# One-bank accumulators, a planner that counts descriptor space, and first weights by ScalarE in a two-layer trunk kernel

## The chip, the cores and the metric

The kernel runs on one core of a Trainium2 chip. The metric is the device time of one execution in microseconds (us), from several runs of the same program. Engines are called as the profile does: PE is the matrix engine (PEld its weight loads), DVE the vector engine, ACT the scalar engine, POOL GpSimd, SP the sync engine, which here only issues DMAs. PSUM is the accumulator memory: eight banks, of 512 f32 values in each of 128 partitions.

## What is computed

The reference is a trunk of two layers on x of 512 rows by 1024 columns in f32, each layer followed by a dense FFN, and a norm at the end:

```python
def sgu_mixer(h, w_in, w_s, b_s, ln_g, ln_b, w_out):
    z = jax.nn.gelu(h @ w_in)
    u, v = jnp.split(z, 2, axis=-1)
    v = layernorm(v, ln_g, ln_b)
    ...
    mixed = jnp.einsum('gts,bcsgd->bctgd', w, v)
    ...
    return (u * mixed) @ w_out

def retention(h, positions, w_in, gn_g, w_out):
    proj = h @ w_in
    q, k, v, g = jnp.split(proj, [RET_QK_WIDTH, 2 * RET_QK_WIDTH,
                                  2 * RET_QK_WIDTH + RET_V_WIDTH], axis=-1)
    ...
    return (o.astype(h.dtype) * jax.nn.silu(g)) @ w_out

def swiglu(h, w_gu, w_down):
    a, b = jnp.split(h @ w_gu, 2, axis=-1)
    return (jax.nn.silu(a) * b) @ w_down
```

Layer 0 mixes by sgu_mixer in chunks of 128 rows and 8 groups, layer 1 by retention with 4 heads, chunk by chunk. Every block reads an RMS-normed copy of x and is added back to x. The FFN's hidden width is 2816.

## The kernel before, in words

**Numbers.** Each f32 operand of a matmul is split in two parts of a shorter format: ACT makes the high part (names wh_, XH, xP7h), DVE the low part as the difference (wl_, XL, xP7l). A product is three matmuls: high by high, low by high, high by low. The large products use Strassen's scheme with seven block products, P1, P7, P6, Q4, P5, P2 and P3 (`seven`, L845). They need sums of weight blocks and sums of blocks of x. A raw weight block (wr_) is loaded by a DMA that SP issues. Where two blocks must be added, DVE does it, or GpSimd issues a second DMA that adds while it writes ("addition" below). Products are accumulated in PSUM under the names X, Y and Z: X_gu is accumulator X of the FFN's first product, X_dn of its second, X_so of the mixer's output product, X_qk and X_vg of retention's projections, X_ro of its output product, ps_v and X_u of the mixer's input products, mix of the spatial product.

**Stages in time.** The projection of v runs to 56 us, then u and the spatial mix to about 115, the mixer's output to 150, the first FFN to 480, retention to 840, the second FFN to 1182, and the last norm and store follow. At a block's opening, x is normed row chunk by row chunk (xs_), PE transposes it into PSUM (`turn`, L1204, tiles xT_), ACT copies the raw turned x (xr_, `raw_copy`, L1269) and its high part (XH_), DVE makes the low part and the sums of blocks, and xA (L1282) makes the high and low parts of those sums (xP7h, xP7l and so on).

**PSUM.** PS (L656) hands out one of four tiles of two banks, and done (L670) gives it back. A two-bank accumulator is written by PE in halves, c = 0 and c = 1, one bank each, and read by DVE or ACT either whole (128x1024) or by halves (128x512). The recorder counts a PSUM tile as one piece (L132, the grain): any write of any bank waits for every earlier read of the tile.

**The order.** No operation is issued when the code calls it. A Recorder (L211, L289: `record`) writes down every operation with its reads, writes and an estimated duration, and a planner (`order_of`, L430; `deadlines` and `forward` behind it) simulates the engines and two DMA lanes, one for SP's and ACT's transfers and one for GpSimd's. In the simulation each engine picks, among operations that are ready, the one that has to be done first; PE takes the lowest number. At most eight transfers per lane are in the air (HW_DMAS). Tiles come from pools with fixed numbers of buffers (N_GEN = 39, N_TMP = 5). The best of several rounds is emitted (L626), and each engine then runs its list strictly in order, with semaphores between engines. Since every operation is emitted by one line, all rows of the profile bear L341, and they are told apart by names.

**The head.** ACT issues one small load, SP the loads of x and of the first weights in turn (`open_w`, L1380). PE runs five warming matmuls on a constant tile (WAKE), then transposes the first block of x (`turn_in`, L1221) and begins with the projection of v (`open_step`, L1392, loop from L1406).

Of the kernel before, what the change touches and what calls it, by code (L numbers as in the profile page):

```python
# [15 lines left out]
P = 128  # L16
T = 512
# [4 lines left out]
KF = FF // P  # L22
HEADS = 4
GROUPS = 8
WAKE = 5
PREP = 5
FETCH = 8
ADD = 8
# [2 lines left out]
HIGH = 6  # L31
SUM = 7
N_GEN = 39
N_TMP = 5
SO = ("P1", "P7", "P6", "Q4", "P5", "P2", "P3")
UO = ("P1", "P7", "P6", "P2", "Q4", "P5", "P3")
U_DMA = ("P7",)
# [79 lines left out]
RESULT = 35  # L117
TO_PE = 55
HW_DMAS = 8


class Virtual:
# [72 lines left out]
        return n  # L195


class Pool:
    def __init__(self, rec, real, bufs, psum):
        self.rec, self.real, self.bufs, self.psum = rec, real, bufs, psum  # L200
# [4 lines left out]

class Op:
    __slots__ = ("n", "engine", "call", "before", "after", "tiles", "new", "busy", "took", "table", "kind", "start", "end",
                 "late", "left", "ready", "ins", "what", "slow", "then", "ahead", "open", "expect")


class Recorder:  # L211
# [11 lines left out]
    def add(self, engine, call, reads, writes, what, busy, took, table=None, kind=None, slow=0):  # L223
        op = Op()
        op.n, op.engine, op.call, op.what, op.busy, op.took, op.table, op.kind = len(self.ops), engine, call, what, busy, took, table, kind
        op.before, op.after, op.then, op.tiles, op.new, op.ins, op.slow, op.ahead = set(), [], [], [], [], None, slow, self.ahead
        seen = set()
        for views, w in ((reads, False), (writes, True)):
            for v in views:
                t, m = v.tile, v.mask()  # L230
                for q, qm, qw in t.history:
                    if q is not op and (w or qw or t.pool.psum and q.engine != engine) and qm & m:
                        op.before.add(q)
                if id(t) not in seen:
                    seen.add(id(t))
                    op.tiles.append(t)
                    t.users.append(op)
                    if t.first is None:
                        t.first = op
                        op.new.append(t)  # L240
                        if t.pool.psum:
                            was = self.held.get(t.tag)
                            self.held[t.tag] = t
                            op.before.update(was.users if was else ())
        for views, w in ((reads, False), (writes, True)):
            for v in views:
                t, m = v.tile, v.mask()
                if w:
                    t.history = [h for h in t.history if h[1] & ~m]
                t.history.append((op, m, w))  # L250
        for q in op.before:
            (q.then if q.engine == engine == "PE" else q.after).append(op)
        self.ops.append(op)
        return op
# [34 lines left out]
def record(self, attr, name, args, kwargs):  # L289
    args = [as_view(a) for a in args]  # L290
    kwargs = {k: as_view(a) for k, a in kwargs.items()}
    writes, reads = [], []
    if "out" in kwargs:
        writes.append(kwargs["out"])
    elif args:
        writes.append(args[0])
    if "accum_out" in kwargs:
        writes.append(kwargs["accum_out"])
    if "accum_op" in kwargs:
        reads.append(args[0])  # L300
    reads += [a for a in args[1:] if isinstance(a, View)]
    reads += [a for k, a in kwargs.items() if isinstance(a, View) and k not in ("out", "accum_out")]
    writes = [w for w in writes if isinstance(w, View)]
    engine = ENGINE_OF[attr]
    table = kind = None
    slow = 0
    n = writes[0].width() if writes else reads[0].width()
    psum = any(r.tile.pool.psum for r in reads)
    if name == "dma_start":
        kind = "add" if "accum_op" in kwargs else "load" if writes else "store"  # L310
        size = n * 4 * (writes or reads)[0].shape[0]
        busy = {"SP": 450, "POOL": 1200, "ACT": 450}[engine]
        took = busy
        slow = max(60, size * (SERVE_ADD if kind == "add" else SERVE) // 524288)
    elif name == "transpose":
        busy, took = 103, 275
    elif engine == "PE":
        n = args[2].width()
        busy = 4 * n // 2.4 if args[2].tile.dtype == F32 else max(60, n / 2.4 + (13.7 if n < T else 14.7))
        busy = int(busy + 0.0)  # L320
        took = busy + 166
    elif engine == "DVE":
        inputs = [r for r in reads if r.width() > 1 or n == 1]
        two = name in ("tensor_tensor", "scalar_tensor_tensor", "bn_stats") or psum
        busy = int(66 + (1.042 if two else 0.524) * (reads[0].width() if name == "bn_stats" else n))
        if name == "scalar_tensor_tensor" and isinstance(args[2], View):
            busy += 60
        took = busy + 84
    elif engine == "ACT":
        func = args[2]  # L330
        busy = int(90 + 0.835 * n) + (95 if "accum_out" in kwargs else 0)
        took = busy + 120 + (95 if "accum_out" in kwargs else 0)
        table = None if func in (AF.Copy, AF.Square) else str(func)
        if isinstance(kwargs.get("scale"), View):
            busy, took = int(88 + 1.03 * n), int(178 + 1.03 * n)
    else:
        busy = took = int(100 + 1.4 * n)
    fn = getattr(getattr(self.real, attr), name)

    def call():  # L340
        return fn(*[real_of(a) for a in args], **{k: real_of(a) for k, a in kwargs.items()})  # L341
    what = f"{name} {(writes or reads)[0].tile.name}"
    return self.add(engine, call, reads, writes, what, busy, took, table, kind, slow)
# [125 lines left out]
def forward(ops):  # L469
# [105 lines left out]
    while events:  # L575
# [7 lines left out]
        for e in queue:  # L583
            while busy_until[e] <= now:
                op = None
                if e == "PE":
                    op = min((o for o in queue[e] if can(o)), key=lambda o: o.n, default=None)
                else:
                    for o in queue[e]:
                        if can(o):  # L590
                            if o.kind:
                                fly = issued["sw" if e == "POOL" else "hw"]
                                if len(fly) >= HW_DMAS and (fly[-HW_DMAS].end is None or fly[-HW_DMAS].end > now):
                                    continue
                            cost = o.late + (3 * TABLE if o.table and o.table != table else 0)
                            if op is None or (cost, o.n) < best:
                                op, best = o, (cost, o.n)
# [35 lines left out]
def trunk(ctx, tc, x, positions, mix_g, ffn_g, fin_g, sgu_w_in, sgu_w_s, sgu_b_s, sgu_ln_g, sgu_ln_b,  # L633
# [19 lines left out]
    def TMP(name):  # L653
        return tmp.tile([P, T], F32, tag="t", name=name)

    ps_free = [0, 1, 2, 3]  # L656
    ps_held = []

    def PS(name, shape=(P, 2, T)):

        s = ps_free.pop(0)
        t = psp.tile(list(shape), F32, tag=f"ps{s}", name=name)
        ps_held.append((t, s))
        return t

    def done(*tiles):

        for t in tiles:
            i = next(i for i, (u, _) in enumerate(ps_held) if u is t)
            ps_free.append(ps_held.pop(i)[1])  # L670

    def f32(t):
        return t.bitcast(F32)
# [18 lines left out]
    onesr = const.tile([P, P], F32R, name="onesr")  # L692
    nc.vector.tensor_copy(onesr, ones)
    nc.scalar.activation(const.tile([P, 1], F32, name="first"), ones[:, 0:1], AF.Gelu_apprx_tanh)
    wake = PS("wake")
    flat = G("flat", F32R)
    nc.vector.tensor_copy(flat[:, 0, :].rearrange("p (c t) -> p c t", t=P), ones.view().rearrange("p (c t) -> p c t", c=1).to_broadcast([P, 4, P]))
    for _ in range(WAKE):
# [13 lines left out]

    def rows_to_cols(name):
        n = rows_in[name].shape[0]
        ps = PS(f"{name}_ps")
        nc.tensor.transpose(ps[:, 0, 0:n], rows_in[name], ident[0:n, 0:n])
        cols = const.tile([P, n], F32, name=f"{name}_cols")
        nc.vector.tensor_copy(cols, ps[:, 0, 0:n])
        done(ps)
        return cols  # L720
# [405 lines left out]
    def rows_of(cols, dst, name):  # L1126
# [2 lines left out]
        nc.vector.tensor_copy(ch, cols)  # L1129
        cl = small.tile([P, NC], F32R, tag="cl", name=f"cl_{name}")  # L1130
        nc.vector.tensor_tensor(cl, cols, f32(ch), ALU.subtract)
        ps = PS(f"rp_{name}")
        for i, part in enumerate((ch, cl)):
            dg = tmp.tile([P, NC, P], F32R, tag="t", name=f"dg{i}_{name}")
            nc.vector.tensor_tensor(
# [84 lines left out]

    def turn_in(c, j):  # L1221

        ps = PS(f"xT_in_{c}_{j}", (P, KD, P))
        for k in range(4):
            turned[c, j] = nc.tensor.transpose(ps[:, k, :], X[:, c, (4 * j + k) * P:(4 * j + k + 1) * P], ident)
        if (c, j) == (0, 0):
# [153 lines left out]
    def open_w(i):  # L1380
        wr = G(f"wr_v0_{i}")
        for a in range(2) if i < 2 else ():
            nc.sync.dma_start(wr[:, a, :], w_in[(2 * i + a) * P:(2 * i + a + 1) * P, D:D + T])
        if i >= 2:
            nc.sync.dma_start(wr, w_in[2 * i * P:(2 * i + 2) * P, D:D + T].rearrange("(a p) n -> p a n", p=P))
        wh, wl = G(f"wh_v0_{i}", F32R), G(f"wl_v0_{i}", F32R)
# [19 lines left out]
    for j in range(2):  # L1406
        for c in range(NC):
            if c == 0:
                open_w(2 * j)
            if (c, j) != (3, 1):  # L1410
                at = (c + 1) % NC, j + (c + 1) // NC
                load_x(*at)
            if c == 1:
                open_w(2 * j + 1)
            if (c, j) != (3, 1):
                turn_in(*at)
            open_step(c, 2 * j)
            if c == 1:
                open_step(0, 2 * j + 1)
            if c >= 1:  # L1420
                open_step(c, 2 * j + 1)
            if j == 1:
                square_in(c)
# [508 lines left out]
```

## Time and profile before

| what | value |
|---|---|
| time, median of 3 runs | 1189.12 us (1188.01 to 1190.46) |
| time of the profiled execution | 1190.77 us |
| its span, first to last instruction | 1189.1 us |
| mean granted clock of PE | 0.996 |
| instructions: PE, DVE, ACT, POOL | 7491, 1172, 851, 153 |
| bytes moved by DMA | 232.99 MB, 196 GB/s on the mean |
| additions (POOL's queue), share of 16 DMA engines | 74.72 MB, 37.7% |
| loads (SP's queue), share of 16 DMA engines | 156.80 MB, 40.3% |

The profiled execution took 1190.77 us by its own time, of which 1.67 us lie outside the span. It is 1.65 us above the median of the runs. The trace gives each instruction's start and duration, and for an engine that stood idle what ended the idle time: "[2.62 <-ACT xP7h_r]" is 2.62 us of idle before the instruction, ended by ACT's instruction that wrote xP7h_r. "issue" as a releaser means that the engine waited for nothing that the profile shows.

### The profile page before, as it was taken

Reading aid. Unit: us, or ns where it says so; the run is one execution under the profiler, and the core shown is the slowest. Engines: PE = TensorE matmul, PEld = TensorE weight load, DVE = VectorE, ACT = ScalarE, POOL = GpSimd, SP = SyncE. Lnnn points to the kernel's source line nnn. Section 1 sums busy time; section 2 is a strip of 40 time slices with the busy share of each in tenths; the row PEclk is TensorE's granted clock in tenths of the full one; section 3 lists DMA queues with packets and bytes.
Section 4 is the critical chain, followed back from the end, with each engine's and each line's share of the span. In section 5 each row is a group of like instructions: output and inputs, shape, how many; then the busy total and the mean of one; then the engine's idle time right before and its main releaser. Section 6 shows DMA issues by size and latency. Waiting matters only on the chain.

```text
span 1189.1 us, 18709 instructions
## 1 busy us (share of the span) xinstructions
PE 1172.1 (99%) x7491; PEld 1066.4 (90%) x7491; DVE 998.9 (84%) x1172; ACT 689.6 (58%) x851; POOL 177.9 (15%) x153
## 2 busy tenths in 40 slices
PE   9999999999999999899999999999999999999997
PEld 7899799989999988788989888888899989999986
DVE  6999999888779799898967678899988887665896
ACT  6445766456443558656656565567675545445474
POOL 1002121201101120211102011120121111011220
PEclk9999999999999999999999999999999999999999
DMA  9449988798856888869766788788897789669892
GB/s 327 114 126 207 310 183 215 167 240 211 214 143 155 192 186 277 193 143 234 163 169 174 162 213 197 168 166 260 240 217 178 166 225 228 180 170 241 177 228 80
DMA packets 132776, 232.99 MB, mean 196 GB/s; under 512 B 7592, under 2 KB 32208, under 8 KB 132688
## 3 DMA queue, kind: packets, MB, share of 16 engines
q1 hardware_dynamic: 91152, 156.80, 40.3%
q0 software_dynamic: 41376, 74.72, 37.7%
q8 instruction: 59, 0.97, 0.3%
q10 hardware_dynamic: 160, 0.27, 0.1%
q14 instruction: 29, 0.24, 0.1%
HBM read 228.61 MB, written 2.10 MB: 194 GB/s over the span
## 4 chain that ended last, share of the span: by engine, by line
PE 71%; DVE 8%; ACT 2%; issue 1%; DMA 1%; DVEq 0%; ACTq 0%
PE X_gu L341 19%; PE Y_gu L341 10%; PE X_dn L341 7%; PE X_vg L341 7%; PE Z_gu L341 4%; PE Y_dn L341 4%; PE X_qk L341 4%; PE Y_vg L341 4%; PE pv L341 2%; PE Y_qk L341 2%; PE Z_dn L341 2%; PE Z_vg L341 1%; DVE X L341 1%; PE sc L341 1%; PE X_ro L341 1%
## 5 line engine op out<-in xcount | busy, mean ns | idle before, releaser
L341 ACT ACTIVATE wh_gu_P<-wr_gu_P 128x1024 fp32r<-128x1024 f32 x132 | 137.3, 1056 | 128.6 <-DVE wr_gu_P L341 40.9
L341 DVE TENSOR_TENSOR wl_gu_P<-wr_gu_P,wh_gu_P 128x1024 fp32r<-128x1024 f32 x132 | 159.7, 1223 | 47.1 <-ACT wh_gu_P L341 39.0
L341 POOL DMA_DIRECT2D wr_gu_P<-in_ffn_w_gu x50 | 60.8, 1245 | 378.9 <-DVE wl_gu_P L341 179.2
L341 ACT ACTIVATE wh_dn_P<-wr_dn_P 128x1024 fp32r<-128x1024 f32 (+1 forms) x72 | 69.3, 983 | 45.7 <-PE Y_gu L341 8.7
L341 DVE TENSOR_TENSOR wl_dn_P<-wr_dn_P,wh_dn_P 128x1024 fp32r<-128x1024 f32 (+1 forms) x72 | 80.2, 1133 | 8.3 <-ACT wh_dn_P L341 7.7
L341 POOL DMA_DIRECT2D wr_dn_P<-in_ffn_w_down x40 | 46.4, 1191 | 173.7 <-DVE wl_dn_P L341 67.0
L341 DVE TENSOR_TENSOR wl_vg_P<-wr_vg_P,wh_vg_P 128x1024 fp32r<-128x1024 f32 x48 | 57.5, 1221 | 8.7 <-ACT wh_vg_P L341 7.6
L341 ACT ACTIVATE wh_vg_P<-wr_vg_P 128x1024 fp32r<-128x1024 f32 x48 | 49.1, 1060 | 18.7 <-DMA wr_vg_P<-in_ret_w_in 10.3
L341 POOL DMA_DIRECT2D wr_vg_P<-in_ret_w_in x26 | 32.1, 1310 | 137.1 <-DVE wl_vg_P L341 69.6
L341 PE MATMUL X_gu<-xP3h_f,wh_gu_P 128*128 128x256 f32 x176 | 50.4, 286 | 0.2 <-DVE s L341 0.2
L341 PE MATMUL Z_gu<-XH_f,wh_gu_P 128*128 128x256 f32 x176 | 50.0, 284 | 0.0
L341 PE MATMUL X_gu<-XH_f,wh_gu_P 128*128 128x256 f32 x176 | 49.9, 284 | 0.0
L341 PE MATMUL Y_gu<-xP7l_f,wh_gu_P 128*128 128x256 f32 x176 | 49.8, 283 | 0.0
L341 PE MATMUL X_gu<-xP6h_f,wh_gu_P 128*128 128x256 f32 x176 | 49.8, 283 | 0.0
L341 PE MATMUL X_gu<-xP6l_f,wh_gu_P 128*128 128x256 f32 x176 | 49.8, 283 | 0.0
L341 PE MATMUL X_gu<-xP6h_f,wl_gu_P 128*128 128x256 f32 x176 | 49.8, 283 | 0.0
L341 PE MATMUL Y_gu<-XL_f,wh_gu_Q 128*128 128x256 f32 x176 | 49.8, 283 | 0.0
L341 PE MATMUL Y_gu<-XH_f,wl_gu_Q 128*128 128x256 f32 x176 | 49.8, 283 | 0.0
L341 PE MATMUL Y_gu<-XH_f,wh_gu_Q 128*128 128x256 f32 x176 | 49.8, 283 | 0.0
L341 PE MATMUL X_gu<-xP5h_f,wh_gu_P 128*128 128x256 f32 x176 | 49.8, 283 | 0.0
L341 PE MATMUL Y_gu<-xP7h_f,wh_gu_P 128*128 128x256 f32 x176 | 49.8, 283 | 0.0
L341 PE MATMUL Y_gu<-xP7h_f,wl_gu_P 128*128 128x256 f32 x176 | 49.8, 283 | 0.0
(676 smaller groups left out, 4374.6 us busy)
## 6 DMA issues: line engine op xcount, KB each, us to landing
wr_gu_P<-in_ffn_w_gu SPq DMA_DIRECT2D x110, 512.0 KB, 5.9
wr_gu_P<-in_ffn_w_gu POOLq DMA_DIRECT2D x50, 512.0 KB, 7.9
wr_dn_P<-in_ffn_w_down SPq DMA_DIRECT2D x50, 512.0 KB, 5.7
wr_vg_P<-in_ret_w_in SPq DMA_DIRECT2D x40, 512.0 KB, 5.5
wr_dn_P<-in_ffn_w_down POOLq DMA_DIRECT2D x33, 512.0 KB, 8.1
wr_vg_P<-in_ret_w_in POOLq DMA_DIRECT2D x26, 512.0 KB, 8.1
wr_qk_P<-in_ret_w_in SPq DMA_DIRECT2D x20, 512.0 KB, 5.4
wr_ro_P<-in_ret_w_out SPq DMA_DIRECT2D x20, 512.0 KB, 6.1
```

The source lines that it names most:

```text
L341: return fn(*[real_of(a) for a in args], **{k: real_of(a) for k, a in kwargs.items()})
```

## The change

The change has six parts.

- **Accumulators of one bank.** PS now has eight one-bank tiles. A two-bank accumulator becomes a Pair of two tiles, and `record` splits each operation that has a Pair among its operands into two operations, one for each bank (`half_of` cuts the other operands). Tiles that never needed more take one bank: the warming tile, the small transposes, and xT_in.
- **Descriptor space.** The program is built with dynamic_dma_scratch_size 4096 instead of 2048.
- **The planner counts it.** Each transfer has a number `ring`: 2 if its last dimension is under 512, else 1. An addition isn't planned while its own number and those of the last seven that haven't finished 300 ns ago come to more than 7.
- **First weights by ScalarE.** The two loads of the first weight block are issued by ACT.
- **Order at the head.** The first step of the first product (`open_step(0, 0)`) is written ahead of the second block's transposes, and there are four warming matmuls instead of five.
- **Room.** N_TMP goes from 5 to 4 (2048 bytes of each partition).

In the built program DVE has 1248 instructions where it had 1174, ACT 869 where it had 803 (two of them DMA issues), SP 320 where it had 322; POOL's number is the same, PE has one matmul less. The diff, without the parts that only pass shapes:

```diff
-WAKE = 5
+WAKE = 4
...
-N_TMP = 5
+N_TMP = 4
...
+RING = 7
+FREED = 300
...
+def half_of(a, i, n):
+    if isinstance(a, Pair):
+        return a.parts[i].view()
+    if isinstance(a, View) and a.width() > 1:
+        assert a.shape[1] == n, (a.shape, n)
+        return a[:, i * n // 2:(i + 1) * n // 2]
+    return a
...
+        op.ring = 2 if kind and writes and writes[0].shape[-1] < T else 1
...
+    both = [a for a in (*args, *kwargs.values()) if isinstance(a, Pair)]
+    if both:
+        for i in range(2):
+            op = record(self, attr, name, [half_of(a, i, both[0].n) for a in args], {k: half_of(a, i, both[0].n) for k, a in kwargs.items()})
+        return op
...
+                                if e == "POOL" and o.ring + sum(q.ring for q in fly[-RING:] if q.end is None or q.end + FREED > now) > RING:
+                                    continue
...
-    ps_free = [0, 1, 2, 3]
+    ps_free = list(range(8))
...
-        s = ps_free.pop(0)
-        t = psp.tile(list(shape), F32, tag=f"ps{s}", name=name)
-        ps_held.append((t, s))
+        size = 1
+        for k in shape[1:]:
+            size *= k
+        banks = [ps_free.pop(0) for _ in range(size // T)]
+        if len(banks) == 1:
+            t = psp.tile(list(shape), F32, tag=f"ps{banks[0]}", name=name)
+        else:
+            t = Pair([psp.tile([P, shape[1] // 2, *shape[2:]], F32, tag=f"ps{b}", name=f"{name}_{i}") for i, b in enumerate(banks)])
+        ps_held.append((t, banks))
...
-            nc.sync.dma_start(wr[:, a, :], w_in[(2 * i + a) * P:(2 * i + a + 1) * P, D:D + T])
+            (nc.sync if i else nc.scalar).dma_start(wr[:, a, :], w_in[(2 * i + a) * P:(2 * i + a + 1) * P, D:D + T])
...
+            if (c, j) == (0, 0):
+                open_step(0, 0)
             if (c, j) != (3, 1):
                 turn_in(*at)
-            open_step(c, 2 * j)
+            if (c, j) != (0, 0):
+                open_step(c, 2 * j)
...
-    nc = bacc.Bacc("TRN2", target_bir_lowering=False, num_devices=1, dynamic_dma_scratch_size=2048)
+    nc = bacc.Bacc("TRN2", target_bir_lowering=False, num_devices=1, dynamic_dma_scratch_size=4096)
```

What the order of the built program shows of this at two places stands in the prediction, beside the sums that use it.

More of the change, by code (lines that the diff above doesn't have):

```diff
@@ L195, in width, with __init__, __getitem__ @@
         return n
+class Pair:
+    def __init__(self, parts):
+        self.parts = parts
+        self.n = 2 * parts[0].dims[1]
+    def __getitem__(self, key):
+        at, h = key[1], self.n // 2
+        if isinstance(at, int):
+            return self.parts[at // h][(key[0], at % h) + tuple(key[2:])]
+        a, b = at.start or 0, self.n if at.stop is None else at.stop
+        if a == 0 and b == self.n:
+            return self
+        i = a // h
+        assert (b - 1) // h == i, key
+        return self.parts[i][(key[0], slice(a - i * h, b - i * h)) + tuple(key[2:])]
+def half_of(a, i, n):
[5 more added lines that the diff above has]
+    return a
 class Pool:
@@ L207 @@
     __slots__ = ("n", "engine", "call", "before", "after", "tiles", "new", "busy", "took", "table", "kind", "start", "end",
-                 "late", "left", "ready", "ins", "what", "slow", "then", "ahead", "open", "expect")
+                 "late", "left", "ready", "ins", "what", "slow", "then", "ahead", "open", "expect", "ring")
 class Recorder:
@@ L669, in done @@
             i = next(i for i, (u, _) in enumerate(ps_held) if u is t)
-            ps_free.append(ps_held.pop(i)[1])
+            ps_free.extend(ps_held.pop(i)[1])
     def f32(t):
@@ L694, in trunk @@
     nc.scalar.activation(const.tile([P, 1], F32, name="first"), ones[:, 0:1], AF.Gelu_apprx_tanh)
-    wake = PS("wake")
+    wake = PS("wake", (P, 1, T))
     flat = G("flat", F32R)
@@ L714, in rows_to_cols @@
         n = rows_in[name].shape[0]
-        ps = PS(f"{name}_ps")
+        ps = PS(f"{name}_ps", (P, 1, T))
         nc.tensor.transpose(ps[:, 0, 0:n], rows_in[name], ident[0:n, 0:n])
@@ L1131, in rows_of @@
         nc.vector.tensor_tensor(cl, cols, f32(ch), ALU.subtract)
-        ps = PS(f"rp_{name}")
+        ps = PS(f"rp_{name}", (P, 1, T))
         for i, part in enumerate((ch, cl)):
@@ L1221, in turn_in @@
     def turn_in(c, j):
-        ps = PS(f"xT_in_{c}_{j}", (P, KD, P))
+        ps = PS(f"xT_in_{c}_{j}", (P, 4, P))
         for k in range(4):
```

## Prediction

> **What bounds the kernel now.** I read the page's busy row first, then the list of waits of the matrix engine, then the timeline round the longest waits. The page's first row, with busy time and share of the span by engine:
>
> ```profile
> PE 1172.1 (99%) x7491; PEld 1066.4 (90%) x7491; DVE 998.9 (84%) x1172; ACT 689.6 (58%) x851; POOL 177.9 (15%) x153
> ```
>
> PE is busy 1172.1 of 1189.1 us. The number of matmuls stays (one warming matmul goes), so the change can win only from the 17.0 us in which PE waits, and from stretches at a low clock; it loses wherever it makes PE wait anew. PE's waits, each with its total, count and longest:
>
> ```profile
> PE Y_qk L341 <- ACT xP7h_r L341: 2.6, 1, 2.6
> PE X_qk L341 <- ACT xP6h_r L341: 1.8, 1, 1.8
> PE wake L341 <- DVE flat L341: 1.7, 1, 1.7
> PE mix L341 <- DVE mx L341: 1.1, 1, 1.1
> PE X_so L341 <- DVE X L341: 0.8, 1, 0.8
> PE X_qk L341 <- ACT rq L341: 0.6, 1, 0.6
> PE X_dn L341 <- DVE X L341: 0.5, 1, 0.5
> PE xT_in L341 <- DMA X<-in_x: 0.4, 1, 0.4
> PE X_gu L341 <- DVE s L341: 0.2, 1, 0.2
> ```
>
> These nine make 9.7 us; of the remaining 7.3 nearly all is the tail behind PE's last matmul (the last row below, ended at 1182.0 of 1189.1). The worst place is the opening of retention, near 500 us. PE's timeline there:
>
> ```profile
> 494.03 1.03 PE L341 MATMUL xT_r<-ident,xs_r 128*128 128x128 f32 x8
> ...
> 503.14 0.58 PE L341 MATMUL Y_qk<-xP7h_r,wh_qk_P 128*128 128x256 f32 x1 [2.62 <-ACT xP7h_r L341]
> 505.54 0.58 PE L341 MATMUL X_qk<-xP6h_r,wh_qk_P 128*128 128x256 f32 x1 [1.82 <-ACT xP6h_r L341]
> 505.92 0.42 PE L341 MATMUL Y_qk<-xP7l_r,wh_qk_P 128*128 128x256 f32 x1
> ...
> 509.55 0.31 PE L341 MATMUL Y_qk<-xP7h_r,wh_qk_P 128*128 128x256 f32 x1
> 509.69 0.28 PE L341 MATMUL Y_qk<-xP7l_r,wh_qk_P 128*128 128x256 f32 x1
> ...
> 510.17 0.28 PE L341 MATMUL Y_qk<-xP7h_r,wl_qk_P 128*128 128x256 f32 x1
> ...
> 1181.65 0.39 PE L341 MATMUL W_dn<-wh_dn_P,h_P3l 128*128 128x512 f32 x1
> ```
>
> PE had turned x by 495.06 (first row), yet the high half of its sum, xP7h_r, came at 503.1. ACT's timeline, DVE's and GpSimd's say why:
>
> ```profile
> 499.19 1.06 ACT L341 ACTIVATE wh_vg_P<-wr_vg_P 128x1024 fp32r<-128x1024 f32 x1 [4.37 <-DMA wr_vg_P<-in_ret_w_in]
> 500.16 1.06 ACT L341 ACTIVATE xr_r<-xT_r 128x512 f32<-128x512 f32 x2
> ...
> 502.03 1.06 ACT L341 ACTIVATE xP7h_r<-xP_r 128x1024 fp32r<-128x1024 f32 x1
> ```
>
> ```profile
> 496.00 1.22 DVE L341 TENSOR_TENSOR wl_vg_P<-wr_vg_P,wh_vg_P 128x1024 fp32r<-128x1024 f32 x1
> 500.77 2.36 DVE L341 TENSOR_TENSOR xP_r<-xr_r,xr_r 128x1024 f32<-128x1024 f32 x2 [3.56 <-ACT xr_r L341]
> 503.17 1.23 DVE L341 TENSOR_TENSOR xP_r<-xP_r,xr_r 128x1024 f32<-128x1024 f32 x1
> 504.31 1.22 DVE L341 SCALAR_TENSOR_TENSOR xP7l_r<-xP_r,xP7h_r 128x1024 fp32r<-128x1024 f32 x1
> ```
>
> ```profile
> 484.07 1.76 POOL L341 DMA_DIRECT2D wr_vg_P<-in_ret_w_in  x1
> 490.21 1.22 POOL L341 DMA_DIRECT2D wr_vg_P<-in_ret_w_in  x1 [4.38 <-issue]
> ```
>
> ACT stood 4.37 us before a weight copy that needed an addition; the two copies of turned x (xr_r), queued behind it, had been ready for 5 us. That addition was issued at 490.21, after GpSimd had been held 4.38 us by something that the profile doesn't name ("issue"), following two additions at 483 and 484. The change counts a 256-wide addition as two units and holds one back when seven would be passed, with the space doubled; before, with half of that, 2+1 units were out. So I read the hold as descriptor space: an inference, not a row.
>
> The cost there is idle time and then clock:
>
> ```profile
> 500.00:504.00 4.00, 1.10 (x4) 0.38 (x2) 3.19 (x3) 3.92 (x6) 1.17 (x1) 0.85 0.96 178
> 504.00:508.00 4.00, 2.46 (x11) 2.46 (x12) 4.00 (x5) 3.15 (x4) 0.00 (x0) 0.50 0.96 204
> 508.00:512.00 4.00, 4.00 (x30) 4.00 (x29) 4.00 (x5) 1.51 (x3) 0.00 (x0) 0.80 0.02 3
> ```
>
> The columns are the stretch, its length, busy time of PE, weight load, DVE, ACT and POOL with counts, then granted clock, DMA share, GB/s: the clock falls to 0.85, 0.50, 0.80. From 505.92 to 509.55 there are 17 matmuls in 3.63 us, 0.214 each; at full clock four take 0.48 (509.69 to 510.17), 0.12 each. The loss is 17 x 0.094 = 1.6 us.
>
> **The change part by part.** *Retention's opening.* The new accounting makes the planner's order different. ACT before, from the first of the copies in question (xr_r copies of turned x, XH_r its high half, wh_ high halves of weights):
>
> ```order
> L341 ACTIVATE wh_vg_P_0_0_5180<-wr_vg_P_0_0_4979 128x1024
> L341 ACTIVATE wh_qk_P_0_0_5193<-wr_qk_P_0_0_4906 128x1024
> L341 ACTIVATE wh_vg_P_0_2_5208<-wr_vg_P_0_2_5020 128x1024
> L341 ACTIVATE xr_r_0_5160<-xT_r_5203 128x4x128
> L341 ACTIVATE xr_r_1_5167<-xT_r_5203 128x4x128
> L341 ACTIVATE XH_r<-xT_r_5203 128x8x128
> L341 ACTIVATE xP7h_r<-xP_r 128x1024
> ```
>
> And now, at the same place:
>
> ```order
> L377 ACTIVATE wh_qk_P_0_0_5292<-wr_qk_P_0_0_4962 128x1024
> L377 ACTIVATE wh_vg_P_0_0_5298<-wr_vg_P_0_0_5062 128x1024
> L377 ACTIVATE xr_r_0_5257<-xT_r_0_5310 128x4x128
> L377 ACTIVATE xr_r_1_5266<-xT_r_1_5315 128x4x128
> L377 ACTIVATE XH_r<-xT_r_1_5315 128x4x128
> L377 ACTIVATE xP7h_r<-xP_r 128x1024
> L377 ACTIVATE xP5h_r<-xP_r 128x1024
> L377 ACTIVATE xP6h_r<-xP_r 128x1024
> L377 ACTIVATE wh_vg_P_0_2_5366<-wr_vg_P_0_2_5118 128x1024
> ```
>
> The copy of the late weights has moved behind all three sums, so x no longer waits for an addition, however late. Next in line is DVE: with xr_r from 495.1 and DVE's low halves of weights done at 497.2, two sums of 1.18 end at 499.4 with xP7h ready 1.06 after the first; a third sum of 1.2 and xP7l's 1.2 end at 501.8. PE comes free at 500.5 (503.14 less 2.62) and its second matmul needs xP7l: 1.2 us stay, and of the wait for rq some 0.3. So 2.6 + 1.8 + 0.6 = 5.0 of idle plus 1.6 of clock are 6.6 now, and 1.5 remain: **-5.1**. If the late addition is still the last to come for a matmul behind it, up to 2.6 remain.
>
> Whether a gap of 1.2 us costs clock, the stretch with mix's gap of 1.1 tells (columns as above):
>
> ```profile
> 72.00:76.00 4.00, 3.48 (x30) 3.48 (x31) 4.00 (x6) 0.00 (x0) 0.00 (x0) 1.00 0.09 19
> ```
>
> The clock stayed at 1.00 there, while after 2.62 and 1.82 it did not. By the Trainium skill, "TensorE: Matmul & The Clock Gate", HAM oscillation, only gaps over about 3.4 us matter; here the clock fell in a stretch whose single waits were 2.62 and 1.82, so the row is stricter. By the page alone I could not have charged the first gap with any clock; the 1.6 us, and the sum, stay as measured.
>
> *One-bank accumulators.* A write to a two-bank tile had to wait for a read of its other bank. PE at X_so before, where the second bank (first row with "wh_so_P_0_0") begins:
>
> ```order
> L341 MATMUL X_so<-wh_so_P_0_2_1347,y_P3h_1369 128x512
> L341 MATMUL X_so<-wl_so_P_0_2_1375,y_P3h_1369 128x512
> L341 MATMUL X_so<-wh_so_P_0_2_1347,y_P3l_1420 128x512
> L341 MATMUL X_so<-wh_so_P_0_0_1322,y_P3h_1369 128x512
> L341 MATMUL X_so<-wl_so_P_0_0_1366,y_P3h_1369 128x512
> ```
>
> And now:
>
> ```order
> L377 MATMUL X_so_1171<-wh_so_P_0_2_1384,y_P3h_1397 128x512
> L377 MATMUL X_so_1171<-wl_so_P_0_2_1434,y_P3h_1397 128x512
> L377 MATMUL X_so_1171<-wh_so_P_0_2_1384,y_P3l_1408 128x512
> L377 MATMUL X_so_1182<-wh_so_P_0_0_1377,y_P3h_1397 128x512
> L377 MATMUL X_so_1182<-wl_so_P_0_0_1391,y_P3h_1397 128x512
> ```
>
> The order is the same; the second bank is a tile of its own, and nothing reads it while DVE adds the first to X. So X_so's 0.8, X_dn's 0.5 and X_gu's 0.2 go. Of mix's 1.1 I count half, 0.6, since DVE's own place for mx can keep the other half. **-2.1**; bounds 0 and -2.6.
>
> *Split instructions.* Built, DVE has 74 more and ACT 64 more (two first loads apart). Durations of whole and half:
>
> ```profile
> L341 DVE TENSOR_TENSOR X<-X,X_dn 128x1024 f32<-128x1024 f32 x9 | 10.9, 1217 | 5.5 <-PE X_dn L341 5.5
> L341 DVE TENSOR_TENSOR X<-X,X_dn 128x512 f32<-128x512 f32 x6 | 3.9, 685 | 0.0
> ```
>
> ```profile
> L341 ACT ACTIVATE y<-Y_gu 128x1024 f32<-128x1024 f32 x10 | 10.2, 1016 | 4.8 <-PE Y_gu L341 4.2 <-PE X_gu L341 0.6
> L341 ACT ACTIVATE rq<-X_qk 128x512 f32<-128x512 f32 x8 | 4.7, 590 | 2.0 <-PE X_qk L341 1.9
> ```
>
> Two halves cost 2 x 0.685 - 1.217 = 0.15 more on DVE, 74 x 0.15 = 11.3 us; on ACT 2 x 0.590 - 1.016 = 0.16, 64 x 0.16 = 10.5 us. DVE then stands at 1010 of 1189 us and ACT at 700, both below PE. DVE is full only in some stretches:
>
> ```profile
> 420.00:450.00 30.00, 30.00 (x134) 24.83 (x133) 29.96 (x30) 19.29 (x22) 5.44 (x5) 1.00 0.90 202
> 450.00:480.00 30.00, 30.00 (x146) 25.15 (x144) 29.32 (x44) 24.48 (x38) 1.32 (x1) 1.00 0.92 274
> ```
>
> In the sixty microseconds before 480 DVE has 0.72 us free and PE does not wait once: DVE prepares weights ahead there. The splits in it are few (by the program five additions of a sum to X), 0.8 us, which the free time about takes. So the splits lie beside PE's work; if the lead is used up, they surface. For new waits of this sort, and those of the altered order, I put in one bank read of 0.7: **+0.7**; bounds 0 and 2.6, as much as the short waits of today.
>
> *Head.* SP's first two weight loads go to ScalarE, one warming matmul goes, and the first step comes before the second turn.
>
> ```profile
> 1.26 0.90 SPq L341 DMA_DIRECT2D wr_v<-in_sgu_w_in  x2
> ```
>
> ```profile
> 5.40 0.63 ACT L341 ACTIVATE wh_v<-wr_v 128x512 fp32r<-128x512 f32 x1 [2.46 <-DMA wr_v<-in_sgu_w_in]
> 6.61 0.63 ACT L341 ACTIVATE wh_v<-wr_v 128x512 fp32r<-128x512 f32 x1 [0.58 <-DMA wr_v<-in_sgu_w_in]
> ```
>
> SP's queue is 0.90 us shorter for the x that follows, so at most 0.9 is won; but these landings are 1.2 apart, and a first weight that lands one place later costs 1.2. ACT's table load moves behind two issues and is covered by the 2.46 of waiting. **0**, bounds -0.9 and +1.2.
>
> *Tail:* its instructions stand as before. **0.**
>
> Sum on the profiled execution, whose time is 1190.77 (the span and 1.67 around it): -5.1 - 2.1 + 0.7 = -6.5, 1184.3. It lay 1.65 above the median of the runs, 1189.12; so I forecast **1182.6**. Bounds: the retention term -6.6 to -4.0, short waits -2.6 to 0, the new ones 0 to +2.6, the head -0.9 to +1.2 each move it alone; taken together, mostly not all at once, 1179 to 1187.
>
> **Rivals.** Differences within 0.2%, 2.4 us, count as no change.
>
> R1, *the stall stays in another dress*: the sums now wait for a chain of DVE work as long as the wait for the addition. For: DVE has four operations between xr_r and xP7l. Against: the rows give 501.8, not 505.5. Only the short waits are won, -2.1 + 0.7: 1187.7.
>
> R2, *all goes*: no residue at retention (-6.6), all short waits (-2.6), the head's 0.9: 1189.1 - 10.1 = 1179.0. For: the chain's residue shrinks if the additions come early and DVE's low halves with them.
>
> R3, *slower: transfers collide*. With twice the descriptors, GpSimd has up to seven additions in the air, against SP's loads on DMA engines that are already at a share of 0.90 to 0.96 in the stretches quoted. If SP's raw weights land later than the lead of the copies, ACT meets a late DMA ahead of something PE needs, as at 499.19, in other places. One such stall, 6.6 us, eats the gain (1189.2); it decides from two on: 1182.6 + 2 x 6.6 = 1195.8. Against: PE waits for a weight's DMA nowhere after the head, and the planner's lanes reckon with sharing.
>
> R4, *DVE becomes the bound*: half of its 11.3 us surface in the full stretches, 5.6: 1188.2. The Trainium skill, "VectorE: DVE Perf Modes", the errata section, says that each instruction pays a fixed extra cost whatever its size; the 0.15 of the rows agrees. Against: PE has no wait for a low half of a weight today.
>
> **How the numbers follow.** Forecast 0.58, R1 0.14, R2 0.11, R3 0.11, R4 0.06. Faster (below 1186.7): 0.58 + 0.11 and 0.02 of R1, 0.71. Slower (above 1191.5): 0.11. Same: 0.18. Forecast's own range is 1179 to 1187; down to R2 and up to R1 and R4 gives 1178.5 to 1188.8, which leaves R3 and edges out.
>
> **What would show it.** Right: in the list of PE's waits xP7h_r and xP6h_r are gone or make under 1.5 us, the clock near 500 us stays at 1.00, ACT's wait for wr_vg stands behind xP6h_r, and X_so and X_dn wait for no DVE X. DVE's busy time is near 1010. Wrong: a new wait of PE on ACT over 2 us, a second dip of the clock, rows of SP's loads with landing times well above those of today, or DVE's xP sums as late as 503.

## The result and the profile after

The changed kernel takes 1179.18 us on the median (six runs, 1177.65 to 1180.06), the kernel before 1189.05 beside it (six runs, 1185.58 to 1193.55): ratio 0.9914, 95% interval 0.9893 to 0.9935. The forecast was 1182.6. The profiled execution took 1179.72 us, its span is 1177.9.

All the waits that PE has left, as its list of waits gives them (total, count, longest), and the page's busy row:

```profile
PE wake L377 <- DVE flat L377: 1.7, 1, 1.7
PE ps_v L377 <- ACT wh_v L377: 0.9, 2, 0.5
PE xT_in L377 <- DMA X<-in_x: 0.9, 1, 0.9
```

```profile
PE 1167.4 (99%) x7490; PEld 1065.1 (90%) x7490; DVE 1009.1 (86%) x1246; ACT 694.3 (59%) x915; POOL 177.4 (15%) x153
```

Of the nine waits shown of before, the seven behind the head are gone, and none has come in their place. All three that are left lie in the first ten microseconds, where one has grown and one is new. DVE works 10.2 us more, about the 11.3 forecast; ACT 4.7 more, not 10.5.

At the opening of retention, ACT, GpSimd, DVE and PE in the timeline of the changed kernel:

```profile
492.32 1.09 ACT L377 ACTIVATE xr_r<-xT_r 128x512 f32<-128x512 f32 x2 [0.25 <-PE xT_r L377]
494.68 1.06 ACT L377 ACTIVATE xP7h_r<-xP_r 128x1024 fp32r<-128x1024 f32 x1 [0.79 <-DVE xP_r L377]
498.05 1.04 ACT L377 ACTIVATE wh_vg_P<-wr_vg_P 128x1024 fp32r<-128x1024 f32 x1
```

```profile
479.38 1.21 POOL L377 DMA_DIRECT2D wr_vg_P<-in_ret_w_in  x1
481.42 1.21 POOL L377 DMA_DIRECT2D wr_vg_P<-in_ret_w_in  x1 [0.83 <-DVE nf_dn L377]
```

```profile
493.43 2.35 DVE L377 TENSOR_TENSOR xP_r<-xr_r,xr_r 128x1024 f32<-128x1024 f32 x2
496.96 1.22 DVE L377 SCALAR_TENSOR_TENSOR xP7l_r<-xP_r,xP7h_r 128x1024 fp32r<-128x1024 f32 x1
```

```profile
491.69 1.03 PE L377 MATMUL xT_r<-ident,xs_r 128*128 128x128 f32 x8
498.01 0.28 PE L377 MATMUL Y_qk<-xP7h_r,wh_qk_P 128*128 128x256 f32 x1
498.24 0.39 PE L377 MATMUL Y_qk<-xP7l_r,wh_qk_P 128*128 128x256 f32 x1
```

ACT copies the turned x at once; the late weights come behind the sums and are copied without a wait. GpSimd's second addition isn't held. PE goes from Z_vg into Y_qk without a gap: xP7l is ready at 498.18, and the matmul that needs it starts at 498.24. The stretches that had a clock of 0.85 and 0.50:

```profile
500.00:504.00 4.00, 4.00 (x36) 4.00 (x35) 4.00 (x5) 3.22 (x6) 0.00 (x0) 1.00 0.90 221
504.00:508.00 4.00, 3.98 (x29) 3.41 (x28) 4.00 (x5) 3.25 (x5) 2.46 (x2) 1.00 0.45 51
```

To see where the time went, I laid PE's matmuls of the two traces beside each other by work done, the warming ones left out and each other one counted with its usual spacing in the traces (0.227 us for 512 columns, 0.12 for 256, 0.11 for 128), and read how much later the changed kernel is at the same amount of work:

| time before, us | changed kernel against before | step |
|---|---|---|
| to 20 | +2.4 | head |
| 20 to 69 | -0.5 | projection of v, first part of u |
| 69 to 76 | -1.5 | mix |
| 142 to 158 | -1.1 | X_so |
| 188 to 203 | -0.4 | X_gu |
| 474 to 490 | -0.9 | X_dn |
| 490 to 528 | -7.3 | opening of retention |
| 543 to 558, 845 to 861 | -0.6 | two small places |
| all else to PE's end | -1.2 | pieces of 0.15 or less |
| PE's end | -11.1 | 1182.0 against 1170.9 |

The rows sum to -11.1. The profiled executions differ by 11.05 us, the medians by 9.9, since the execution profiled of before was one of its longer ones.

### The profile page after: what moved, and what is told of

The parts are those of the page before. It is cut to its first block, busy times and chain, and to the rows that moved or that the text cites. A ratio compares the mean times of both kernels' runs of the same rounds, so it can differ in the third digit from the quotient of the medians.

```text
span 1177.9 us, 18861 instructions
## 1 busy us (share of the span) xinstructions
PE 1167.4 (99%) x7490; PEld 1065.1 (90%) x7490; DVE 1009.1 (86%) x1246; ACT 694.3 (59%) x915; POOL 177.4 (15%) x153
## 4 chain that ended last, share of the span: by engine, by line
PE 98%; ACT 1%; DMA 1%; DVE 0%; ACTq 0%; issue 0%; DVEq 0%
PE X_gu L377 22%; PE Y_gu L377 11%; PE X_dn L377 9%; PE X_vg L377 7%; PE Z_gu L377 5%; PE Y_dn L377 5%; PE ps_v L377 4%; PE X_qk L377 4%; PE Y_vg L377 4%; PE X_ro L377 4%; PE Z_dn L377 3%; PE pv L377 2%; PE Y_qk L377 2%; PE X_u L377 2%; PE X_so L377 2%; PE Y_ro L377 2%
## 5 line engine op out<-in xcount | busy, mean ns | idle before, releaser
L377 ACT ACTIVATE wh_vg_P<-wr_vg_P 128x1024 fp32r<-128x1024 f32 x48 | 49.7, 1056 | 10.2 <-DMA wr_vg_P<-in_ret_w_in 3.5
L377 PE MATMUL X_gu<-xP5h_f,wl_gu_P 128*128 128x256 f32 x176 | 49.8, 283 | 0.0
L377 PE MATMUL X_gu<-xP3l_f,wh_gu_P 128*128 128x256 f32 x176 | 49.8, 283 | 0.0
L377 PE MATMUL X_gu<-xP3h_f,wl_gu_P 128*128 128x256 f32 x176 | 49.8, 283 | 0.0
```

## The experiments

Theory: the stall at retention's opening needs both, an addition that comes late because descriptor space is full, and a planner's order that puts ACT's copy of these weights ahead of the copies of x; one-bank tiles end the short waits. Rivals: descriptor space alone carries the gain, or the counting does; and for the head, the early first step rather than ScalarE's loads. Each group of four runs shared a chip and its runs of the kernel before.

**Space and order apart (runs 1 to 3).** The kernel before, with nothing but its descriptor space changed; all its instructions stand in the same order:

```diff
-dynamic_dma_scratch_size=2048
+dynamic_dma_scratch_size=2560
```

> The kernel before, instruction for instruction, with descriptor space 2560 instead of 2048 (the most that fits beside its other buffers). If GpSimd's hold of 4.38 us near 486 us is descriptor space, one more addition fits: the addition that came at 490.2 comes near 486, ACT does not wait 4.37 us for it, PE's waits for xP7h_r and xP6h_r (2.6 + 1.8) fall below 1.5 together, the clock dip goes, and the time is 5 to 7 us under the kernel before. If the hold is something else (the rival: the order alone decides), all of this stays as before and the time is within 1 us of the kernel before.

Measured: 1185.65 us against 1188.72 for the kernel before on that chip (29 runs, 1183.4 to 1192.9), ratio 0.998 (0.9963 to 0.9997). GpSimd's timeline, and two of PE's waits:

```profile
485.56 2.44 POOL L341 DMA_DIRECT2D wr_vg_P<-in_ret_w_in  x2 [5.61 <-DVE wl_vg_P L341]
```

```profile
PE X_gu L341 <- ACT u L341: 2.0, 2, 1.0
...
PE X_qk L341 <- ACT xP6h_r L341: 1.1, 1, 1.1
```

Two additions now follow each other at once: the hold was descriptor space, as nothing else differs. The wait for xP7h_r is gone and that for xP6h_r is 1.1. Laid side by side by work done, PE gains 5.6 us from 490 to 528. Less than that shows in the times. The profiled execution is 2.6 below the one profiled before, since new or longer waits in the FFNs take back 3.1 us, of which the two for u make 2.4. The median is 3.1 below, since the kernel before doesn't always have the full stall: of its 29 runs here, the ten with a mean granted clock of 0.996 or less all took 1189.99 or more, and the ten with 0.998 or 0.999 took 1183.4 to 1186.5. In runs 1 to 3 none of the 30 executions is under 0.997.

The kernel before with only the pool of temporaries made smaller, with which the planner's order comes out with the late copy behind the sums of x:

```diff
-N_TMP = 5
+N_TMP = 4
```

> The kernel before with only N_TMP 4 instead of 5: descriptor space stays 2048, nothing is counted, banks and head as before. The planner's order then happens to have the late weight copy behind the three sums of x. If the order is what ends the stall, PE's waits for xP7h_r and xP6h_r make under 1.5 us while GpSimd is still held for about 4 us near 486, and the time is 5 to 7 us under the kernel before. The rival, that the addition's lateness matters wherever the copy stands, expects PE to wait 2 us or more for a part of wr_vg or a chain behind it, and a time within 2 us of the kernel before.

Measured: 1185.10, ratio 0.9979 (0.9961 to 0.9997). GpSimd's row and PE's wait:

```profile
491.88 1.22 POOL L341 DMA_DIRECT2D wr_vg_P<-in_ret_w_in  x1 [5.74 <-issue]
```

```profile
PE X_qk L341 <- ACT xP6h_r L341: 1.4, 1, 1.4
```

The hold is there, longer than before (5.74 against 4.38), and the stall is not: this order without more space is enough too. The prediction put the new order down to the counting; nothing was counted here, so it can come about without. The smaller pool may have moved other instructions as well; runs 11 and 12 move one alone. Both edits together:

```diff
-N_TMP = 5
+N_TMP = 4
-dynamic_dma_scratch_size=2048
+dynamic_dma_scratch_size=4096
```

> The same instructions in the same order as the run with N_TMP 4, with descriptor space 4096. If order alone ends the stall, the time is within 1 us of that run, and only GpSimd's hold near 486 goes. If space matters beside it (the rival), it is 2 us or more below that run.

Measured: 1185.26, ratio 0.9975 (0.9957 to 0.9992), the same as with the order alone. The wait for xP6h_r falls to 0.2 in the profiled execution, which the medians do not show. All three lie 3.1 to 3.6 us under the median of before, not 5 to 7: the mechanism came as expected, but the expected size was that of the execution profiled before, which had the full stall (run 3's profiled one, of 1184.50, is 6.3 below it), and not that of the median one.

**Head (runs 4 to 7).** The changed kernel with its head as before:

```diff
-WAKE = 4
+WAKE = 5
-            (nc.sync if i else nc.scalar).dma_start(wr[:, a, :], w_in[(2 * i + a) * P:(2 * i + a + 1) * P, D:D + T])
+            nc.sync.dma_start(wr[:, a, :], w_in[(2 * i + a) * P:(2 * i + a + 1) * P, D:D + T])
-            if (c, j) == (0, 0):
-                open_step(0, 0)
...
-            if (c, j) != (0, 0):
-                open_step(c, 2 * j)
+            open_step(c, 2 * j)
```

> The changed kernel with the head as before: five warming matmuls, first weights by SP, first step behind the second turn. By the comparison of the two traces PE in the changed kernel is 2.0 to 2.6 us later from 20 to 66 us. If the three edits of the head cost that, PE reaches the end of the first projection 2 us earlier and the time is 1.5 to 2.5 us below the changed kernel, near 1177. The rival, that the one-bank tiles of the turned x or the altered order cost it, expects no difference above 0.5 us.

Measured: 1176.33, ratio to the kernel before 0.9909 (0.9889 to 0.9929). That is 2.85 us below the 1179.18 of the changed kernel, which was not measured beside it. In the two profiled executions, side by side by work done, the changed kernel is 4.1 later, all of it by 14 us. The changed kernel ran again beside the next three:

> The changed kernel once more, unedited, so that the head's edits are compared on one chip: near 1179.

Measured: 1178.67, ratio 0.991 (0.9892 to 0.9928). Then each of two edits undone by itself; the first weights issued by SP:

```diff
-            (nc.sync if i else nc.scalar).dma_start(wr[:, a, :], w_in[(2 * i + a) * P:(2 * i + a + 1) * P, D:D + T])
+            nc.sync.dma_start(wr[:, a, :], w_in[(2 * i + a) * P:(2 * i + a + 1) * P, D:D + T])
```

> The changed kernel with the first weights issued by SP again, in SP's turn between the loads of x; four warming matmuls and the early first step stay. If the loads by ScalarE cost the head its time, because x and weights then share the DMA engines and the first weight copy starts at 6.9 us instead of 5.4, this is 1.5 to 2.5 us below the changed kernel. The rival, that the early first step costs it by putting PE's transposes behind a wait for weights, expects less than 0.7 us.

Measured: 1177.41, ratio 0.99 (0.9882 to 0.9917), 1.3 below the changed kernel beside it, which is between what the theory and its rival expected. And the first step behind the second turn:

```diff
-            if (c, j) == (0, 0):
-                open_step(0, 0)
...
-            if (c, j) != (0, 0):
-                open_step(c, 2 * j)
+            open_step(c, 2 * j)
```

> The changed kernel with the first step behind the second turn again; first weights by ScalarE and four warming matmuls stay. If the loads by ScalarE are what costs, less than 0.7 us below the changed kernel. If the early first step is (the rival), 1.5 to 2.5 us below.

Measured: 1180.03, ratio 0.9921 (0.9901 to 0.9941), its runs from 1176.24 to 1180.59. The median is 1.4 above the changed kernel, where both theories expected it below. ACT's first weight copy in the timelines of the changed kernel, of its second run, with the loads by SP, and with the step back:

```profile
6.93 0.63 ACT L377 ACTIVATE wh_v<-wr_v 128x512 fp32r<-128x512 f32 x1 [3.13 <-DMA wr_v<-in_sgu_w_in]
```

```profile
6.25 0.63 ACT L377 ACTIVATE wh_v<-wr_v 128x512 fp32r<-128x512 f32 x1 [2.46 <-DMA wr_v<-in_sgu_w_in]
```

```profile
5.17 0.63 ACT L377 ACTIVATE wh_v<-wr_v 128x512 fp32r<-128x512 f32 x1 [2.22 <-DMA wr_v<-in_sgu_w_in]
```

```profile
6.51 0.63 ACT L377 ACTIVATE wh_v<-wr_v 128x512 fp32r<-128x512 f32 x1 [2.71 <-DMA wr_v<-in_sgu_w_in]
```

Issued by ScalarE the first weights come 1.1 to 1.8 us later than issued by SP in its turn. The Trainium skill, "DMA: Bandwidth & Descriptors", Issuing engines are not separate DMA queues, says that transfers run on the same 16 engines and interleave whoever issues them, so that only issue time is saved; in these rows the weights land later all the same. What is shown is that the three edits together cost 2 to 3 us (runs 4 and 9 against the result and run 5, on chips whose medians of the kernel before lie within 1.3) and that undoing ScalarE's loads alone wins 1.3 of them. Why, stays open: with the step back the weights come late as well (6.51), and that execution, of 1176.24, is as fast as any with the head put back, while one other of the same program took 1178.6 and four took about 1180. Neither theory foresaw this, and none of the five has a profile. The mean granted clocks on record give a hint: with ScalarE's loads (result, runs 5 and 7) 9 of 18 executions show 0.997 or less, with SP's (runs 4, 6, 8 to 10 and 12) all 36 show 0.998 or more. No profile is of one of the nine, so where their clock is lost is not shown.

**Banks alone (run 8).** The run with the head put back, without the rest:

```diff
-N_TMP = 4
+N_TMP = 5
-                                if e == "POOL" and o.ring + sum(q.ring for q in fly[-RING:] if q.end is None or q.end + FREED > now) > RING:
+                                if False and e == "POOL" and o.ring + sum(q.ring for q in fly[-RING:] if q.end is None or q.end + FREED > now) > RING:
-dynamic_dma_scratch_size=4096
+dynamic_dma_scratch_size=2048
```

> Only the one-bank accumulators: head, N_TMP 5 and descriptor space 2048 as before, nothing counted. The planner's order here also has the late weight copy behind the sums of x. If one-bank tiles give the short waits (mix, X_so, X_gu, X_dn: some 4 us with the restarts) and the order ends the stall, this lies within 1.5 us of the run with the head put back, near 1177, though GpSimd is held for some us again. If the descriptor space carries the gain (the rival), it is 4 us or more above that run.

Measured: 1176.70, ratio 0.9895 (0.9877 to 0.9914), 2.0 below the changed kernel on the same chip. One-bank accumulators alone, with the order that the planner makes of them, give the whole gain and more.

What the one-bank tiles are worth beside order and space, runs 3 and 4 tell, on one chip: run 3 has the late copy behind the sums, the space and two-bank tiles, run 4 has one-bank tiles and the counting, which by run 8 isn't needed. Their medians are 1185.26 and 1176.33, so 8.9 us. PE's waits behind the head in run 3:

```profile
PE mix L341 <- DVE mx L341: 1.1, 1, 1.1
PE X_dn L341 <- DVE X L341: 0.9, 1, 0.9
PE X_so L341 <- DVE X L341: 0.8, 1, 0.8
PE X_gu L341 <- ACT u L341: 0.6, 1, 0.6
PE X_qk L341 <- ACT rq L341: 0.6, 1, 0.6
...
PE X_qk L341 <- ACT xP6h_r L341: 0.2, 1, 0.2
```

Run 4 has none behind the head. By work done, run 4's profiled execution gains 7.6 us on run 3's behind the head: 1.5 at mix, 1.1 at X_so, 0.9 in the first FFN's first product, 1.2 at X_dn, 0.7 at retention's opening, and the rest in pieces under 0.45.

**One instruction moved (runs 9 to 12).** The base, the head put back:

> The changed kernel with the head put back, once more, as the base of the three runs beside it: near 1176.5.

Measured: 1176.14, ratio 0.9891 (0.9867 to 0.9916). With the old descriptor space and the same order of instructions:

```diff
-dynamic_dma_scratch_size=4096
+dynamic_dma_scratch_size=2048
```

> The same instructions in the same order as the run with the head put back, with descriptor space 2048 as before. If, once the late copy stands behind the sums of x, descriptor space is worth nothing, it is within 0.7 us of that run, though GpSimd is held again near 480 us. The rival, that the doubled space carries part of the gain, expects 2 us or more above it.

Measured: 1176.54, ratio 0.9894 (0.9868 to 0.9921). GpSimd's row, and ACT's copy of the late weights:

```profile
481.29 1.22 POOL L377 DMA_DIRECT2D wr_vg_P<-in_ret_w_in  x1 [3.75 <-DVE nf_dn L377]
```

```profile
494.97 1.04 ACT L377 ACTIVATE wh_vg_P<-wr_vg_P 128x1024 fp32r<-128x1024 f32 x1
```

GpSimd stood idle for 3.75 us ahead of the addition. The row names nf_dn as the releaser, but in run 9, the same program with 4096, this addition starts 2.8 us earlier, at 478.48. Still nobody waits for it: the copy comes at its turn. Now one instruction of ACT is put where it stood before the change, ahead of the two copies of turned x, with 2048 and with 4096:

```diff
-        for op in order_of(rec):
+        ops = order_of(rec)
+        i = next(i for i, op in enumerate(ops) if op.engine == "ACT" and op.what.endswith(" xP7h_r"))
+        xr = [j for j in range(i) if ops[j].engine == "ACT" and " xr_r_" in ops[j].what][-2]
+        late = next(j for j in range(i, len(ops)) if ops[j].engine == "ACT" and " wh_vg" in ops[j].what)
+        ops.insert(xr, ops.pop(late))
+        for op in ops:
             op.call()
```

> Descriptor space 2048 and the head put back, and one instruction moved: ScalarE's copy of the late weights stands ahead of the two raw copies of turned x, as in the kernel before. If the place of that copy together with the held addition made the stall, it comes back with one-bank tiles too: PE waits 3 to 5 us for xP7h_r and what follows, the clock falls below 1, and the time is 3 to 7 us above the run without the move. If one-bank tiles, or anything else in the new order, ended the stall (the rival), the time is within 1 us of it.

Measured with 2048: 1181.13, ratio 0.9922 (0.9893 to 0.995); four runs at 1180.7 to 1181.9, two at 1176.0 and 1177.3. In the profiled execution, of 1181.94, GpSimd, ACT, PE's waits and the stretches (columns as in the prediction):

```profile
484.51 1.22 POOL L377 DMA_DIRECT2D wr_vg_P<-in_ret_w_in  x1 [5.53 <-DVE xs_r L377]
```

```profile
492.87 1.06 ACT L377 ACTIVATE wh_vg_P<-wr_vg_P 128x1024 fp32r<-128x1024 f32 x1 [3.07 <-DMA wr_vg_P<-in_ret_w_in]
```

```profile
PE Y_qk L377 <- DVE xP7l_r L377: 2.1, 1, 2.1
...
PE Y_qk L377 <- ACT xP7h_r L377: 0.9, 1, 0.9
```

```profile
496.00:500.00 4.00, 1.13 (x6) 0.93 (x7) 3.97 (x4) 3.72 (x4) 1.09 (x1) 0.95 0.83 118
500.00:504.00 4.00, 4.00 (x24) 4.00 (x24) 4.00 (x5) 0.79 (x3) 0.00 (x0) 0.62 0.67 190
```

The stall of before is back, with the lower clock, in a kernel with one-bank tiles and no other wait behind the head. And with 4096:

> The same one instruction moved, with descriptor space 4096. The addition comes some 8 us earlier, so ScalarE finds it landed and loses only its own 1.0 us: within 1.5 us of the run with the head put back. If the move alone makes the stall whatever the addition does (the rival), as far above as with 2048.

Measured: 1176.20, ratio 0.9891 (0.9867 to 0.9915). The rows:

```profile
477.30 1.20 POOL L377 DMA_DIRECT2D wr_vg_P<-in_ret_w_in  x1 [0.82 <-DVE nf_dn L377]
```

```profile
486.91 1.99 ACT L377 ACTIVATE wh_vg_P<-wr_vg_P 128x1024 fp32r<-128x1024 f32 x2
```

The addition comes 7.2 us earlier, and ACT copies it without a wait. So place and lateness are needed together: 1176.1, 1176.5 and 1176.2 without the one or the other, 1181.1 with both. Of the latter, the two runs of 1176.0 and 1177.3 have a mean granted clock of 0.998, the four others 0.996 to 0.997, so the stall, as in the kernel before, seems not to come in every execution; the two have no profile.

## Why the prediction was right, and where not

**Retention's opening, -5.1; measured -7.3.** The mechanism was right: ACT's copy of late weights ahead of x, the held addition, the idle time and then the clock. Three things were not. First, the cause of the new order: the counting isn't needed for it. A smaller pool (run 2) and one-bank tiles (run 8) each bring the late copy behind the sums by themselves; the counting alone was not run. Second, the residue of 1.5: none is left. I let DVE's low halves of weights end 2.1 us after the last transpose (497.2 against 495.06), as in the trace of before; in the changed kernel the sums start 0.7 us after it (493.43 against 492.72), so xP7l comes in time. Third, the price of a wait, below.

**Short waits, -2.1; measured -3.9** (mix 1.5, X_so 1.1, X_gu 0.4, X_dn 0.9). All went, mix's whole. I had counted only half of mix, and for all four I took the idle time that the list of waits gives, which is too little. PE's timeline at X_so before:

```profile
146.30 0.39 PE L341 MATMUL X_so<-wh_so_P,y_P3l 128*128 128x512 f32 x1
147.47 0.50 PE L341 MATMUL X_so<-wh_so_P,y_P3h 128*128 128x512 f32 x1 [0.78 <-DVE X L341]
147.81 0.40 PE L341 MATMUL X_so<-wl_so_P,y_P3h 128*128 128x512 f32 x1
```

And in the changed kernel:

```profile
146.31 0.39 PE L377 MATMUL X_so<-wl_so_P,y_P3h 128*128 128x512 f32 x1
146.54 0.40 PE L377 MATMUL X_so<-wh_so_P,y_P3l 128*128 128x512 f32 x1
```

In a stream one matmul starts 0.23 after the last, though each is shown 0.39 long. Across the wait it is 1.17, then 0.34 to the next: 1.17 + 0.34 - 2 x 0.23 = 1.05 lost, where the list says 0.78. These four waits cost 0.2 to 0.4 more each than their rows.

**Split instructions and new waits, +0.7; measured 0.** DVE's 10.2 us more stayed beside PE's work; no wait behind the head is left. ACT's 64 instructions more cost 4.7, not 10.5. I had taken two halves as twice one alone, but those that follow each other overlap: two xr_r of 128x512 take 1.09 together in the row at 492.32, where a whole copy took 1.02. 64 x 0.07 would be 4.5, which fits, though how many of the 64 follow their other half was not counted.

**Head, 0 with a bound of +1.2; measured +2.4** in the profiled execution, and 2 to 3 us by medians (1178.7 and 1179.2 against 1176.1 to 1176.7). I priced one landing later; PE was held for the next block of x as well, by 0.9 where before it was 0.4, and twice for weights. A bound from one trace was too narrow, since the same head differs from execution to execution: runs 2 and 3 have the same instructions in the same order, and against the kernel before PE was 1.8 later at 17 us in run 2 and 0.7 earlier in run 3.

**The rivals.** R1 did not come: the chain of DVE work was in time. R2 came nearest: all waits behind the head went, but the head's gain was a loss, so that its 1179.0 was met by misses that cancel. R3 and R4 did not come; SP's loads and DVE's splits made PE wait nowhere behind the head.

The sum went from -6.5 forecast to -11.1 in the profiled execution: -2.2 at retention, -1.8 at the short waits, -0.7 for new waits, +2.4 at the head, and -2.3 in small places that I had not counted. That 1179.2 lies in the range, just above its lower end of 1179, is in part luck: the loss at the head hid some of the rest, and with the head put back the kernel takes 1176.1 to 1176.3, below every bound that I gave.

By the medians the weights of the two main terms are the other way round. Order and space win 3.1 to 3.6 (runs 1 to 3; 4.6 between runs 10 and 11) where I had 5.1, since I took the stall from an execution that had all of it; one-bank tiles win 8.9 (run 3 to run 4) where I had 2.1.

## What to carry to other kernels

An engine that runs its list in order passes on whatever its next instruction waits for: before giving more space to what comes late, see what is queued behind the instruction that needs it, for here moving one copy was worth 4.6 us by the medians of runs 10 and 11, and the space, with the copy in front, 4.9 (runs 11 and 12). Where one engine writes a tile by halves and another reads it, two tiles in its place are worth a trial: here that was the larger part of the gain, though each wait that it took away was 1.1 us or less by its row. When a planner makes the order, any edit may move that copy, so a gain in such a kernel belongs to an edit only once the edit has been tried with the order held. Price a wait of the matrix engine from start to start of its matmuls, and a step's gain against the spread of the runs, not against one profile.

## What the runs showed of the hardware

A single wait of PE of 1.4 us (run 2) left its granted clock at 1.00. Waits of 0.9 and 2.1 with one matmul between them brought it to 0.62 in the next stretch (run 11), and waits of 2.6 and 1.8 with one matmul between to 0.50 (before). Whether the longest wait or the sum counts, these runs don't separate. GpSimd's hold before the addition went when dynamic_dma_scratch_size rose from 2048 to 2560, with every instruction in its place (run 1). A stall that depends on when a DMA lands can make a kernel uneven: on one chip the runs of before spread over 9.5 us, and their mean granted clock goes from 0.999 at the short end to 0.994 to 0.996 at the long one; with the late copy first (run 11) there are two separate groups, 1176 to 1177 and 1181 to 1182. The runs of the changed kernel spread over 2.4 us.
